# Strassen's seven products in the feed-forward of a decoder layer, with features on partitions from the output projection on

## The chip, the cores and the metric

The kernel runs on one core of a Trainium2 chip. A core has a matrix engine (PE, with its weight loads shown as PEld), a vector engine (DVE), a scalar engine (ACT), a general engine (POOL) and SP, which here only issues transfers. They run at the same time, each through its own queue of instructions in order, and wait for each other by semaphores. Operands lie in a memory of 128 partitions (SBUF); PE writes into another (PSUM). The metric is the device time of one execution in microseconds; the number given is the median of the runs.

## The reference

One decoder layer over 1024 tokens of width 1024, in fp32:

```python
n = rms_norm(h, g_mix)
# projections of n, latent attention o_a, stick-breaking attention o_b
merged = sigmoid(gate_a) * (o_a @ w_br_mla) + sigmoid(gate_b) * (o_b @ w_br_sb)
h = h + merged @ w_out                                              # output projection
n2 = rms_norm(h, g_ffn)
h = h + (silu(n2 @ w_ffn_gate) * (n2 @ w_ffn_up)) @ w_ffn_down      # feed-forward, inner width 2816
e = rms_norm(p @ w_ple_proj, g_ple)                                 # per-layer embedding, p is 1024 x 256
h = h + sigmoid(h @ w_ple_gate) * e
return rms_norm(h, g_final)
```

## The kernel before

Every large product is made from fp32r operands of two parts. `split` (L102) writes the high part with a cast on ACT and the rest with a subtraction on DVE; `passes` (L106) issues three matmuls for each block of 128 inner rows: high by high, high by low, low by high. A matmul has 128 inner rows, 128 output rows and 512 output columns.

The stages follow each other: norm, input projections and stick-breaking attention up to about 562 us; latent attention up to about 820; the gated merge (`pb`); the output projection (`po`); then norm, feed-forward and per-layer embedding. From the output projection on, tokens lie on the partitions: `hres` is [128, 8 token tiles, 1024 features]. Since a product needs its inner dimension on the partitions, `transposed` (L124) turns tiles by 4 transposes on PE at a time (`tp`), and splits them: the normalised state before the feed-forward (`n2T`), the state and `p` before the per-layer embedding.

The feed-forward runs over 22 chunks of 128 inner features, in groups of 3, 4, 4, 4, 4 and 3. `gate_up` (L842) loads a column block of each weight, makes `pg` and `pu` for both halves of the tokens with 24 matmuls each, applies Silu on ACT and the product on DVE and splits the result into `gT`, which stays in SBUF. `down` (L860) then multiplies the group's `gT` with its rows of `w_ffn_down` for each token tile into `pd`, and DVE adds `pd` to `hres` (L866). The per-layer embedding follows the last group by three token tiles: `ple_e` (projection `pp`, its norm, transposes) and `ple` (gate product, addition, final norm, store).

The order of the instructions on each engine is set by the framework's scheduler, which simulates times and honours the priorities and the numbers of buffers given for each tile name (`bufs`); SP issues nearly all loads and stores, in order, and one that waits holds back those behind it. POOL issues the stores of the gates and branches and does powers, some multiplications and sums. PSUM has eight banks of 128x512, handed out in turn.

Of the kernel before, what the change touches and what calls it, by code (L numbers as in the profile page):

```python
# [10 lines left out]
F32 = mybir.dt.float32  # L11
# [40 lines left out]
def decoder_layer(ctx: ExitStack, tc: tile.TileContext, x, p, positions, g_mix, w_in, g_q_a, w_q_b,  # L52
                  g_kv_a, w_kv_b, w_br_mla, w_br_sb, w_out, g_ffn, w_ffn_gate, w_ffn_up, w_ffn_down,
                  w_ple_gate, w_ple_proj, g_ple, g_final, out):
    nc = tc.nc
    x, p, out = x[0], p[0, 0], out[0]
# [16 lines left out]
    d_oT = dram.tile([2, 512, S], F32, name="d_oT")  # L73
    d_freq = dram.tile([1, 64], F32, name="d_freq")
    d_rope = dram.tile([64, S], F32, name="d_rope")

# [4 lines left out]
    ident_r = const.tile([P, P], F32R, name="ident_r")  # L81
# [7 lines left out]
    incl = const.tile([P, P], F32R, name="incl")  # L89
    rest = const.tile([P, P], F32R, name="rest")  # L90
    mask_sb = const.tile([P, P], F32R, name="mask_sb")
    mask_mla = const.tile([P, P], F32R, name="mask_mla")

    def tri(tmpm, t, base_val, fill, sign, base):
        # base_val where sign * (row - column) + base >= 0, fill elsewhere
# [10 lines left out]
    def passes(ps, prods, first=True, last=True):  # L106
        n = len(prods)
        for i, ((ah, al), (bh, bl)) in enumerate(prods):
            nc.tensor.matmul(ps, lhsT=ah, rhs=bh, start=first and i == 0, stop=False)  # L109
            nc.tensor.matmul(ps, lhsT=ah, rhs=bl, start=False, stop=False)  # L110
            nc.tensor.matmul(ps, lhsT=al, rhs=bh, start=False, stop=last and i == n - 1)  # L111
# [12 lines left out]
    def transposed(ps_pool, spec, src, dst_h, dst_l, n):  # L124
        # src [128, n*128] -> dst[:, 0:n, :] split
        for c in range(0, n, 4):
            m = min(4, n - c)
            tp = ps_pool.tile([P, 512], F32, name="tp", **spec())
            for i in range(m):
                nc.tensor.transpose(tp[:, i * P:(i + 1) * P], src[:, (c + i) * P:(c + i + 1) * P], ident)  # L130
            tv = tp[:, 0:m * P].rearrange("p (a b) -> p a b", b=P)
            nc.scalar.copy(out=dst_h[:, c:c + m, :], in_=tv)
            nc.vector.tensor_tensor(out=dst_l[:, c:c + m, :], in0=tv, in1=r32(dst_h[:, c:c + m, :]),
                                    op=ALU.subtract)
# [845 lines left out]
```

## Time and profile before

| | |
|---|---|
| median of 3 runs | 1811.73 us (1811.12 to 1811.78) |
| profiled execution, span | 1810.5 us |
| PE busy | 1761.1 us, 97% |
| DVE, ACT, POOL busy | 957.4, 766.6, 219.2 us |
| last matmul of the merge, about | 862 us |
| output projection | 862 to 953 us |
| first gate product | 955 us |
| last matmul of the kernel starts | 1798.7 us |

The profile is of one execution of its own; its span is 1.2 us below the median of the timed runs. A row of a group reads: line, engine, operation, output tile from input tiles, shape, count, then busy time and the mean of one in ns, then idle time of that engine ahead of it and what ended it. A row of the timeline begins with start and duration in us. The slices cut the span into 40 parts of 45.3 us, one digit each, in tenths of the time.

### The profile page before, as it was taken

The page shows a single profiled execution, that of the slowest core. Times are in us where ns is not written, and L with a number is a line of the kernel's source. Part 1 is how long each engine was busy: PE and PEld are TensorE (multiplying, and loading weights), DVE is VectorE, ACT ScalarE, POOL GpSimd, SP SyncE. Part 2 cuts the span into 40 slices and gives each one's busy share as a digit, 9 for nine tenths or more (in the row PEclk, how much of TensorE's full clock was granted, in tenths as well). Part 3 has the DMA queues.
Part 4 walks back from the last instruction along what each step waited for, and adds up shares of the span by engine and source line. Part 5 has one row for each costly group of instructions (what it writes and reads, how often), then busy time and mean ns, then how long its engine had stood idle before and what let it go on. Part 6 is the DMA issues. An engine that isn't in the chain of part 4 may idle for free.

```text
span 1810.5 us, 21501 instructions
## 1 busy us (share of the span) xinstructions
PE 1761.1 (97%) x8224; PEld 1453.3 (80%) x8224; DVE 957.4 (53%) x1641; ACT 766.6 (42%) x1467; POOL 219.2 (12%) x328
## 2 busy tenths in 40 slices
PE   6999999999998999998999999999999999999997
PEld 5888878888786888875888888888888888888885
DVE  6676788777885667777633232232232322325443
ACT  5275677766775767776323111021021021013332
POOL 2021220000211433334100000000000000000111
PEclk9999999999999999999999999999999999999998
DMA  5211122213315111217531111021021021112011
GB/s 169 65 58 42 53 59 59 65 50 97 105 42 158 54 59 36 65 47 268 179 112 57 47 59 47 24 70 47 24 70 49 22 82 51 38 64 91 30 41 39
DMA packets 124377, 126.31 MB, mean 70 GB/s; under 512 B 14130, under 2 KB 100146, under 8 KB 124274
## 3 DMA queue, kind: packets, MB, share of 16 engines
q1 hardware_dynamic: 118242, 105.02, 19.2%
q0 software_dynamic: 6032, 19.93, 3.1%
q8 instruction: 64, 1.05, 0.2%
q14 instruction: 39, 0.32, 0.1%
HBM read 100.54 MB, written 23.60 MB: 69 GB/s over the span
## 4 chain that ended last, share of the span: by engine, by line
PE 59%; DVE 3%; issue 3%; ACT 2%; DMA 1%; POOL 1%; POOLq 0%; SPq 0%; DVEq 0%; ACTq 0%
PE pg L109 5%; PE pg L110 5%; PE pg L111 5%; PE pu L111 4%; PE pu L109 4%; PE pu L110 4%; PE pd L110 4%; PE pd L109 4%; PE pd L111 4%; PE tp L621 2%; PE po L110 1%; PE po L111 1%; PE po L109 1%; PE pb L109 1%; PE op L628 1%
## 5 line engine op out<-in xcount | busy, mean ns | idle before, releaser
L109 PE MATMUL pt<-nTh,w_h 128*128 128x512 f32 (+1 forms) x480 | 192.9, 403 | 3.3 <-ACT go L325 2.1
L110 PE MATMUL pt<-nTl,w_h 128*128 128x512 f32 (+1 forms) x480 | 190.4, 397 | 0.0
L111 PE MATMUL pt<-nTh,w_l 128*128 128x512 f32 (+1 forms) x480 | 189.4, 396 | 0.0
L103 ACT CAST w<-raw 128x1024 fp32r<-128x1024 f32 x73 | 75.0, 1047 | 262.5 <-PE pd L111 166.9
L104 DVE TENSOR_TENSOR w<-raw,w 128x1024 fp32r<-128x1024 f32 x73 | 88.4, 1223 | 135.7 <-ACT w L103 135.7
L856 DVE TENSOR_TENSOR sl<-pu,sl 128x512 f32<-128x512 f32 x44 | 30.4, 692 | 207.0 <-PE pu L111 207.0
L866 DVE TENSOR_TENSOR hres<-pd,hres 128x512 f32<-128x512 f32 x96 | 66.1, 690 | 137.8 <-PE pd L111 137.7
L111 PE MATMUL pg<-n2T,w 128*128 128x512 f32 x352 | 137.2, 390 | 0.0
L110 PE MATMUL pg<-n2T,w 128*128 128x512 f32 x352 | 137.2, 390 | 0.0
L109 PE MATMUL pg<-n2T,w 128*128 128x512 f32 x352 | 137.2, 390 | 0.0
L111 PE MATMUL pu<-n2T,w 128*128 128x512 f32 x352 | 137.2, 390 | 0.0
L109 PE MATMUL pd<-w,gT 128*128 128x512 f32 x352 | 137.2, 390 | 0.0
L111 PE MATMUL pd<-w,gT 128*128 128x512 f32 x352 | 137.1, 389 | 0.0
L110 PE MATMUL pu<-n2T,w 128*128 128x512 f32 x352 | 137.1, 389 | 0.0
L109 PE MATMUL pu<-n2T,w 128*128 128x512 f32 x352 | 137.1, 389 | 0.0
L110 PE MATMUL pd<-w,gT 128*128 128x512 f32 x352 | 137.1, 389 | 0.0
L115 POOL TENSOR_SCALAR rstd<-ms 128x1 f32<-128x1 f32 x32 | 7.5, 235 | 873.1 <-DVE ms L886 766.0
L109 PEld LDWEIGHTS pt<-nTh,w_h 128*128 128x128 f32 (+1 forms) x480 | 90.3, 189 | 26.0 <-ACT go L325 5.0
L111 PEld LDWEIGHTS pt<-nTh,w_l 128*128 128x128 f32 (+1 forms) x480 | 90.4, 188 | 20.4
L855 ACT ACTIVATE sl<-pg 128x512 f32<-128x512 f32 x44 | 26.3, 598 | 190.0 <-PE pg L111 190.0
L110 PEld LDWEIGHTS pt<-nTl,w_h 128*128 128x128 f32 (+1 forms) x480 | 90.5, 189 | 18.7
L607 POOL TENSOR_SCALAR pw<-pw,st 128x128 f32<-128x128 f32 (+5 forms) x48 | 75.5, 1580 | 71.3 <-DVE st L603 24.8
(333 smaller groups left out, 4154.4 us busy)
## 6 DMA issues: line engine op xcount, KB each, us to landing
w_raw<-w_in SPq DMA_DIRECT2D x33, 512.0 KB, 4.2
raw<-w_ffn_gate SPq DMA_DIRECT2D x22, 512.0 KB, 3.9
raw<-w_ffn_up SPq DMA_DIRECT2D x22, 512.0 KB, 3.9
raw<-w_ffn_down SPq DMA_DIRECT2D x22, 512.0 KB, 3.6
d_gate<-go POOLq DMA_DIRECT2D x32, 256.0 KB, 2.6
sg<-d_gate SPq DMA_DIRECT2D x16, 512.0 KB, 4.4
xt<-x SPq DMA_DIRECT2D x8, 512.0 KB, 5.3
d_br<-bo POOLq DMA_DIRECT2D x16, 256.0 KB, 2.4
```

Source lines behind the costliest of these rows:

```text
L103: nc.scalar.copy(out=h, in_=src)
L104: eng.tensor_tensor(out=l, in0=src, in1=r32(h), op=ALU.subtract)
L109: nc.tensor.matmul(ps, lhsT=ah, rhs=bh, start=first and i == 0, stop=False)
L110: nc.tensor.matmul(ps, lhsT=ah, rhs=bl, start=False, stop=False)
L111: nc.tensor.matmul(ps, lhsT=al, rhs=bh, start=False, stop=last and i == n - 1)
L115: nc.gpsimd.tensor_scalar(out=r, in0=ms, scalar1=EPS, scalar2=None, op0=ALU.add)
L607: nc.gpsimd.tensor_scalar(out=pw[:, 0:nk], in0=pw[:, 0:nk], scalar1=st[:, 6:7], scalar2=None, op0=ALU.mult)
L621: nc.tensor.transpose(tp[:, i * P:(i + 1) * P], rows[i][:, kb * P:(kb + 1) * P], ident)
L628: nc.tensor.matmul(op[:, c0:], lhsT=vst[:, kb, :], rhs=tl[:, c0:], start=False, stop=kb == last, skip_group_check=True)
L855: nc.scalar.activation(out=sl, in_=pg, func=AF.Silu)
L856: nc.vector.tensor_tensor(out=sl, in0=pu, in1=sl, op=ALU.mult)
L866: nc.vector.tensor_tensor(out=hres[:, t, cs], in0=pd, in1=hres[:, t, cs], op=ALU.add)
```

## The change

The layout is turned: from the merge on, features lie on the partitions and tokens in the columns, so `hres` is [128, 8 feature blocks, 1024 tokens]. The input x is also given transposed (`xT`), `p` only transposed (`pT`), and the output leaves transposed; the host turns it. All 144 transposes behind the attention go. The attention itself is unchanged.

- **Norms.** Sums over features are now sums over partitions. ACT squares each `hres` block, DVE sums the squares into `acc`, four one-column matmuls with a column of ones make the sum per token (`rstd_cols`, tile `pm`), POOL takes the power. `spread` turns that into a 128x512 tile in PSUM that holds the factor of each token in all partitions (`bc`), by four DVE operations and one fp32 matmul. The three gains are loaded as [128, 8] columns at the very start of the kernel.
- **Output projection.** The same 384 matmuls with operands exchanged. `hres` is loaded from `xT` ahead of it; the result is also stored to DRAM (`d_h`), since the norm overwrites `hres` in place.
- **Embedding projection** (`pp`, 96 matmuls) moves from the end to behind the output projection and is stored to DRAM (`d_e`).
- **Gate and up.** The weight's two blocks of 128 columns and two halves of the inner dimension, and the state's two halves of the inner dimension and of the tokens, make 2x2 blocks each. `right_factors` forms the state's sums once and splits all seven right-hand factors (`b1` to `b7`); `left_sums` forms a unit's four weight sums (`ws`) on POOL; `wino` splits each of seven left-hand factors (`wl`) and makes seven products of 12 matmuls in three PSUM tiles (1, 6, 7 and 4 are summed up in `pP`, 5 and 3 in `pQ`, 2 stands in `pR`), which ACT copies and DVE and POOL additions combine. 22 units of 84 matmuls replace 22 chunks of 96. The SwiGLU outputs (`c`) go to DRAM (`d_g`).
- **Down.** The same with the inner dimension in four groups of 2 x 3, 2 x 3, 2 x 3 and 2 x 2 blocks. For each group `hidden_factors` reloads pieces of `d_g` (`g`), forms differences on POOL (`t`, or in place in `g`) and splits them into tiles `b`, of which there are nine (`g` has ten, `t` four); four `down_unit`s each make seven products of 9 (last group 6) matmuls and add the results to `hres`: three through an ACT copy and a POOL addition, four by DVE from PSUM. `hres` is reloaded from `d_h` first.
- **End.** All of `hres` is split, then 16 gate products of 24 matmuls, the additions and squares, the final norm for each half of the tokens, and the stores.

```diff
+    gains = const.tile([P, 3, NK], F32, name="gains")
+    for gi, g in enumerate((g_ffn, g_ple, g_final)):
+        nc.sync.dma_start(out=gains[:, gi, :], in_=g.rearrange("o (k p) -> p (o k)", p=P))
...
+        for k in range(NK):
+            nc.sync.dma_start(out=hres[:, k, :], in_=xT[k * P:(k + 1) * P, :])
+        for k in range(4, NK):
+            wo_unit(wob, "woB", k, ew.tile([P, D], F32, name="raw", tag="raw", bufs=2))
...
+    def left_sums(sp, raw, nk, wide=4):
+        a11, a12, a21, a22 = blk(0, 0), blk(0, 1), blk(1, 0), blk(1, 1)
+        nc.gpsimd.tensor_tensor(out=s1, in0=a21, in1=a22, op=ALU.add)
+        nc.gpsimd.tensor_tensor(out=s2, in0=s1, in1=a11, op=ALU.subtract)
+        nc.gpsimd.tensor_tensor(out=s4, in0=a12, in1=s2, op=ALU.subtract)
+        nc.gpsimd.tensor_tensor(out=s3, in0=a11, in1=a21, op=ALU.subtract)
+        return {1: a11, 2: a12, 3: s4, 4: a22, 5: s1, 6: s2, 7: s3}
+    def right_factors(sp, dst, kk, b11, b12, b21, b22):
+        nc.gpsimd.tensor_tensor(out=t1, in0=b12, in1=b11, op=ALU.subtract)
+        nc.vector.tensor_tensor(out=t2, in0=b22, in1=t1, op=ALU.subtract)
+        nc.gpsimd.tensor_tensor(out=t3, in0=b22, in1=b12, op=ALU.subtract)
+        nc.vector.tensor_tensor(out=t4, in0=b21, in1=t2, op=ALU.subtract)
+        for i, src in ((5, t1), (6, t2), (7, t3), (3, b22), (4, t4)):
+            split(dst[i][:, 0, kk, :], dst[i][:, 1, kk, :], src)
+    ORDER = (1, 5, 2, 6, 7, 3, 4)
+    def wino(sp, left, right, nk, seen, wide=4):
+        def product(ps_t, i, first):
+            w = sp.tile([P, 2, wide, P], F32R, name="wl", tag="wl", bufs=3)
+            split(w[:, 0, 0:nk, :], w[:, 1, 0:nk, :], left[i])
+            passes(ps_t, [((w[:, 0, k, :], w[:, 1, k, :]), (right[i][:, 0, k, :], right[i][:, 1, k, :]))
+                          for k in range(nk)], first=first, last=i in (2, 3, 4), skip_group_check=True)
...
+            def done(f, t, c):
+                nc.sync.dma_start(out=d_g[(2 * j + f) * P:(2 * j + f + 1) * P, hcol(t)], in_=c)
...
+                if what in ("M1", "U2", "M5"):
+                    s[what] = wk.tile([P, HALF], F32, name="u", tag="u", bufs=3)
+                    nc.scalar.copy(out=s[what], in_=pt)
+                elif what == "C21":
+                    c = sl[1, 0]
+                    nc.vector.tensor_tensor(out=c, in0=pt, in1=c, op=ALU.mult)
+                    done(1, 0, c)
+                else:
+                    nc.vector.tensor_tensor(out=u, in0=pt, in1=u, op=ALU.add)
+                    nc.gpsimd.tensor_tensor(out=sl[key], in0=sl[key], in1=u, op=ALU.mult)
+                    done(*key, sl[key])
...
+                if what in ("M1", "U2", "M5"):
+                    nc.scalar.copy(out=s, in_=pt)
+                    nc.gpsimd.tensor_tensor(out=h, in0=s, in1=h, op=ALU.add)
+                else:
+                    nc.vector.tensor_tensor(out=h, in0=pt, in1=h, op=ALU.add)
+        for nk in (3, 3, 3, 2):
+            Bg = hidden_factors(k0, nk)
+            for j in range(4):
+                yield down_unit(j, k0, nk, Bg)
...
-    def transposed(ps_pool, spec, src, dst_h, dst_l, n):
-            def gate_up(fc):
-            def down(t, gTs, wd):
-            def ple_e(t):
-            def ple(t, e, hT):
```

The order on DVE between the output projection and the first products of the feed-forward, first before. `n2T` is the transposed state, `sl` and `gT` the feed-forward's values, L104 the subtraction of `split`:

```order
1181 L133 TENSOR_TENSOR n2T_9323<-tp,n2T_9323 128x4x128 x3
1182 L791 SCALAR_TENSOR_TENSOR gT<-hres,rstd,gf 128x1024
1183 L133 TENSOR_TENSOR n2T_9323<-tp,n2T_9323 128x4x128 x5
1184 L856 TENSOR_TENSOR sl<-pu,sl 128x512
1185 L104 TENSOR_TENSOR gT<-sl,gT 128x512
1186 L104 TENSOR_TENSOR w<-raw,w 128x1024
1187 L856 TENSOR_TENSOR sl<-pu,sl 128x512
1188 L104 TENSOR_TENSOR w<-raw,w 128x1024
```

In the change, the same place. L929 and L937 scale `hres` by gain and norm factor, L116 is the subtraction of `split`, L847 and L849 are DVE's sums in `right_factors`; `b_9598`, `b_9600` and `b_9603` are the factors `b1`, `b2` and `b3`:

```order
1192 L929 SCALAR_TENSOR_TENSOR hres<-hres,gains,bc 128x512 x8
1193 L116 TENSOR_TENSOR b_9598<-hres,b_9598 128x512
1194 L116 TENSOR_TENSOR wl<-raw,wl 128x512
1195 L116 TENSOR_TENSOR b_9598<-hres,b_9598 128x512 x3
1196 L116 TENSOR_TENSOR b_9600<-hres,b_9600 128x512 x4
1197 L937 SCALAR_TENSOR_TENSOR hres<-hres,gains,bc 128x512 x8
1198 L847 TENSOR_TENSOR ts<-hres,ts 128x512
1199 L116 TENSOR_TENSOR b_9603<-hres,b_9603 128x512
```

And further on in the same queue of the change, the last of 28 such sums and splits, up to the second product (`b_9599`, `b_9601`, `b_9602` and `b_9604` are `b5`, `b6`, `b7` and `b4`):

```order
1220 L847 TENSOR_TENSOR ts<-hres,ts 128x512
1221 L116 TENSOR_TENSOR b_9599<-ts,b_9599 128x512
1222 L849 TENSOR_TENSOR ts<-hres,ts 128x512
1223 L116 TENSOR_TENSOR b_9601<-ts,b_9601 128x512
1224 L116 TENSOR_TENSOR b_9602<-ts,b_9602 128x512
1225 L116 TENSOR_TENSOR b_9604<-ts,b_9604 128x512
1226 L116 TENSOR_TENSOR wl<-ws,wl 128x512
```

Before, eight subtractions stand between the last norm operation and the first value of the feed-forward. In the change the first left-hand factor's subtraction (`wl<-raw`) stands behind eight scalings and a split, and that of the second product (`wl<-ws` in the last row) behind all scalings, sums and splits of the right-hand factors.

The order on SP where the weights of the last group of down are issued, before. `raw` is a weight as loaded:

```order
140 L834 DMA raw<-w_ffn_gate 128x8x128
141 L834 DMA raw<-w_ffn_up 128x8x128
142 L836 DMA raw<-w_ffn_down 128x1024 x3
143 L929 DMA raw<-g_ple 128x1024
144 L934 DMA raw<-w_ple_proj 128x2x512 x2
145 L943 DMA raw<-w_ple_gate 128x2x512 x2
```

And in the change, from the last loads of gate and up to the first of down. `c` is a SwiGLU output, `g` a reloaded piece of it:

```order
155 L922 DMA raw<-w_ffn_gate 128x8x256
156 L975 DMA d_g<-c 128x512 x3
157 L922 DMA raw<-w_ffn_up 128x8x256
158 L975 DMA d_g<-c 128x512 x8
159 L1013 DMA g<-d_g 128x512 x15
160 L1047 DMA raw<-w_ffn_down 128x6x128
161 L1013 DMA g<-d_g 128x512 x2
162 L1047 DMA raw<-w_ffn_down 128x6x128
163 L1013 DMA g<-d_g 128x512 x3
```

Before, down's weights are loads like any others and depend on free buffers alone. In the change the last eight stores of `c`, and 15 reloads, stand ahead of down's first weights.

542 lines of the change are left out of this document (319 added, 223 removed).

## The prediction

> **What bounds the kernel now.** I read the head of the page first (busy time, slices, chain), then windows of the stages that the change touches, then single rows for prices.
>
> ```profile
> span 1810.5 us, 21501 instructions
> PE 1761.1 (97%) x8224; PEld 1453.3 (80%) x8224; DVE 957.4 (53%) x1641; ACT 766.6 (42%) x1467; POOL 219.2 (12%) x328
> PE   6999999999998999998999999999999999999997
> POOL 2021220000211433334100000000000000000111
> PE 59%; DVE 3%; issue 3%; ACT 2%; DMA 1%; POOL 1%; POOLq 0%; SPq 0%; DVEq 0%; ACTq 0%
> ...
> 820.00:870.00 50.00, 43.67 (x184) 33.52 (x183) 42.09 (x53) 30.96 (x40) 22.85 (x8) 1.00 0.80 276
> 870.00:955.00 85.00, 84.65 (x393) 69.93 (x392) 38.38 (x45) 23.53 (x35) 5.24 (x13) 1.00 0.44 136
> 1000.00:1200.00 200.00, 200.00 (x884) 165.63 (x883) 59.44 (x74) 31.27 (x41) 0.00 (x0) 1.00 0.17 50
> ```
>
> PE bounds it nearly everywhere; in the windows the columns are length, PE, PEld, DVE, ACT and POOL busy, granted clock, DMA share, GB/s. A typical stretch of the feed-forward has PE busy for 200 of 200 us and POOL for none. So a matmul removed there is time removed, and nothing there waits yet. One matmul costs its spacing, not its record:
>
> ```profile
> 1100.09 0.39 PE L110 MATMUL pg<-n2T,w 128*128 128x512 f32 x1
> 1100.32 0.39 PE L111 MATMUL pg<-n2T,w 128*128 128x512 f32 x1
> ...
> 928.71 1.47 PE L130 MATMUL tp<-ident,raw 128*128 128x128 f32 x12
> 929.94 0.48 PE L109 MATMUL po<-w,mT 128*128 128x512 f32 x1
> 930.26 0.39 PE L110 MATMUL po<-w,mT 128*128 128x512 f32 x1
> ```
>
> 200/884 gives 0.226 us a matmul. Twelve transposes and the product matmul behind them run from 928.71 to about 930.26, so a transpose takes (1.55 − 0.23)/12 = 0.11 us.
>
> **What is removed.** Of 2112 matmuls each, gate and up keep 22 units of 7 × 12 = 1848 together instead of 2112, and down 3 × 252 + 168 = 924 instead of 1056. That is 264 + 132 = 396 fewer: 396 × 0.226 = −89.6 us. The 144 transposes go: −15.8. Six single-pass fp32 products of 128x512 (`bc`) and 24 tiny ones are new: between 0.23 and four times that each, taken at the top, since fp32 isn't the split format: +5. PE's work falls by 100 us. All of it becomes time only if the other engines keep up; from here I price where they don't.
>
> **Prices for the other engines.**
>
> ```profile
> 838.17 4.28 POOL L738 TENSOR_TENSOR bb<-bb,sg 128x1024 f32<-128x1024 f32 x1 [6.86 <-ACT sg L734]
> 838.32 0.68 DVE L104 TENSOR_TENSOR wl<-raww,wh 128x512 fp32r<-128x512 f32 x1
> 838.92 0.68 DVE L104 TENSOR_TENSOR mT<-sg,mT 128x512 fp32r<-128x512 f32 x1
> 839.52 0.69 DVE L104 TENSOR_TENSOR wl<-raww,wh 128x512 fp32r<-128x512 f32 x1
> ...
> L738 POOL TENSOR_TENSOR bb<-bb,sg x8: 2394/2712/4284, 825.9 to 868.1; 128x1024 f32<-128x1024 f32 x8
> L744 DVE TENSOR_TENSOR sg<-sg,bb x16: 679/680/2896, 828.4 to 872.2; 128x512 f32<-128x512 f32 x16
> L345 POOL TENSOR_TENSOR sqa<-sqa,go x6: 1287/1294/1622, 124.0 to 230.0; 128x512 f32<-128x512 f32 x6
> L103 ACT CAST gT<-sl 128x512 fp32r<-128x512 f32 x44 | 27.2, 618 | 111.3 <-DVE sl L856 111.3
> L325 ACT COPY go<-pt 128x512 f32<-128x512 f32 x42 | 24.3, 578 | 20.6 <-PE pt L111 20.5
> L906 ACT ACTIVATE sg<-raw 128x512 f32<-128x512 f32 x16 | 10.1, 630 | 23.5 <-DVE raw L905 23.5
> L356 POOL TENSOR_TENSOR r<-r,mhalf 128x4 f32<-128x4 f32 x4 | 4.8, 1193 | 0.3
> L890 DVE SCALAR_TENSOR_TENSOR raw<-pp,rstd,raw 128x512 f32<-128x512 f32 x16 | 11.3, 747 | 8.0 <-POOL rstd L116 8.0
> L423 DVE TENSOR_TENSOR al<-sz,ah 128x384 fp32r<-128x384 f32 x16 | 8.9, 555 | 0.5
> L423 DVE TENSOR_TENSOR al<-sz,ah 128x256 fp32r<-128x256 f32 x16 | 6.7, 419 | 0.7 <-PE op L426 0.5
> ```
>
> The first four rows are the important ones. Three DVE subtractions with both operands in SBUF start 0.60 us apart, undisturbed, and the POOL sum beside them takes 4.28 us where its fastest twin takes 2.39: 1.89 longer, three times 0.6. In the other direction L744 takes 2.90 instead of 0.68 us where a POOL sum was ahead of it. So a POOL operation and a two-input DVE operation on SBUF exclude each other, and their times add. I call this sum the port time. Prices: POOL 128x512 1.29 us, DVE 0.60. Between 1.29 and 2.39 (128x1024) a line gives POOL 1.01 for 128x384 and 0.74 for 128x256; DVE takes 0.47 and 0.33 (555 and 419 ns, less the 0.09 by which a record is longer than the spacing).
>
> [...]
>
> **Start.** Three loads of gains with 4-byte elements are put first on SP's queue, ahead of the first `xt`, for which the first transpose waits.
>
> ```profile
> 3.23 3.44 SPq L155 DMA_DIRECT2D w_raw<-w_in  x2
> 6.72 3.83 SPq L262 DMA_DIRECT2D gcol<-g_q_a  x1
> ```
>
> 1024 pieces of w_in hold the queue for 1.72 us, 384 four-byte pieces for 3.83; each new load has 1024. Bounds 0 (the queue takes them quickly) and 12 (3 × 3.83); by piece count 3 × 1.72 = +5.
>
> **Merge to output projection.** The loads of `w_out` k=4 to 7 now stand behind 4 MB of `hres` from xT, which wait for the last merge product.
>
> ```profile
> raw<-w_out SPq DMA_DIRECT2D x8, 512.0 KB, 7.3
> xt<-x SPq DMA_DIRECT2D x16, 256.0 KB, 3.0
> out<-raw SPq DMA_DIRECT2D x16, 256.0 KB, 2.2
> ```
>
> At the 276 GB/s of the 820 to 870 window, 4 MB take 15 us, then 7.3 for a load and 2 for its split. The five output tiles that can begin on the first half of k give PE 60 × 0.226 = 13.6 us of cover, and the merge's tail uses some more. Bounds 2 and 12; I take +4.
>
> **Output projection to the first feed-forward products (A).** In the window 870 to 955 PE has 84.65 of 85 us, so before there is no stall here. Now, after the last output product, come the 16 projections `pp`: PE needs 96 × 0.226 = 21.8 us, but each passes two-deep buffers and takes ACT a cast of half a row (0.35), a copy (0.58) and a square (0.63): 16 × 1.56 = 25 on ACT, and with the filling of the first about 30. Their results go to `d_e` by SP; that and the 16 stores to `d_h` are 8 MB in a stretch with the DMA engines at 0.44, and nothing waits for them until the per-layer embedding. Then DVE's queue holds, in order: 8 scalings (0.69 each, 5.5), 9 subtractions (5.4), 8 scalings (5.5), and 28 two-input operations (16.8) that build the right-hand factors, all ahead of the weight subtraction of the *second* product. POOL's eight differences and the first weight sums share the port with these: +8. With the norm chain (copy 0.58, square 0.63, POOL's sum 1.29, then two short steps: 3.2), the broadcast (1) and the second product's sum, cast and subtraction (2.6) that is 78 us, of which PE works 26.5. So +51. Bounds: 38 (POOL hidden, projections at PE's pace) and 60.
>
> **Gate and up (B).** A pair of units is 168 matmuls, 38.0 us. Port: 11 POOL operations × 1.29 + 14 DVE subtractions × 0.60 = 22.6. DVE's seven additions with one operand in PSUM (0.6 each) bring its own time with all waits for the port to 27; ACT's 14 casts, 6 copies and 4 Silu are 15. All fit into 38. New on SP are the 88 stores to `d_g`, which wait for POOL's products and hold back the weight loads behind them; those have three buffers and are due a whole unit (19 us) later, so I cost them at nothing, and they come into the open once POOL is a unit late. The U2 to U3 reuse of a bank is covered by one product of 2.7 us, as long as DVE is not caught behind POOL twice. Bounds 0 and 15; +5.
>
> **Down (C).** A group of nk=3 is 252 matmuls, 57.0 us. POOL does 12 differences and 12 additions to `hres` (24 × 1.29 = 31.0) and 16 weight sums (16 × 1.01 = 16.2); DVE 21 splits (12.6) and 28 weight splits (28 × 0.47 = 13.2); its 16 additions with an operand in PSUM don't count. Port: 73 us, more than PE. The nk=2 group: POOL 20 × 1.29 + 16 × 0.74 = 37.6, DVE 8.4 + 9.2 = 17.6, together 55 against 38.0. The four groups take 3 × 73 + 55 = 274 us; PE needs 209. At the start the last d_g store waits for the last product, 15 reloads stand behind it on SP, then the first weights: store 2.2, load 3.0, split and first operations about 5, with PE idle; at the end an addition. With these 11 us and 2 for the last additions, +78. Bounds: +17 if POOL and DVE did not exclude each other (only the start and the burst of each new group remain), +100 if the nine `b` buffers push the building of a group into the last unit of the one before.
>
> **End.** The 16 splits of `hres` start only after the last additions: +3. After the last product there are now norm, broadcast, eight scalings through three buffers and eight stores.
>
> ```profile
> 1798.69 0.39 PE L111 MATMUL pg<-wpg,gT 128*128 128x512 f32 x1
> 1804.25 0.81 SPq L917 DMA_DIRECT2D out<-raw  x2
> ```
>
> Before, 11.8 us pass from the last product to the end of the span. Norm chain 5 (square, addition, POOL's power 1.19, three hand-overs), broadcast 2, 8 × 0.69, store 2.2 and 3 of waits for the buffers make 18: +7 (bounds 3 and 12).
>
> **Sum** against the profiled span: 1810.5 − 100.4 + 5 + 4 + 51 + 5 + 78 + 3 + 7 = 1863. The median of the runs is 1811.73, 1.2 above the span; I forecast 1864 us.
>
> **Rivals.**
> 1. *The port doesn't decide down.* If what the rows show is peculiar to the merge's 128x1024 operands, and POOL's sums run beside DVE's subtractions, POOL needs 47 and DVE 35 us of PE's 57 in a group of nk=3, and PE sets the pace again. It decides once a group's 73 falls below 57. Then C is 17 instead of 78 and A loses its 8: 1795, faster. For it speaks that only few rows show the collision; against it, that they show it in both directions and by the full duration.
> 2. *Everything is hidden*, the starts too: 1811.7 − 100 + about 15 for start and end = 1726. It needs A below 10, where DVE's queue alone is 33 us; nearly excluded.
> 3. *Worse:* short waits at each product lower the granted clock, or DVE's additions from PSUM stand behind blocked subtractions so that waits add instead of overlapping, in gate and up too. At 7% more in gate, up and down (423 + 287 us as forecast) it is 1914. Against it: in the window 820 to 870 PE idles 6.3 of 50 us and the clock stays 1.00. [...]
>
> **Chances.** Forecast 0.64, rival 1 0.20, rival 2 0.04, rival 3 0.12. The forecast's own range is 1830 to 1890. For 8 in 10 I go down to rival 1 and up past the upper bounds: 1785 to 1900. Differences within 0.2% (3.6 us) can't be told from no change: faster 0.24, same 0.03, slower 0.73.
>
> **What would show it.** Right: POOL busy some 35 to 60% from gate/up on; a hole of 45 us in PE between the output projection and the second gate product; `hres<-s` and `t<-g` on POOL well above 1.29 us; a group of down taking about 73 us with PE below 80%; gate and up at 38 us a pair. Wrong: PE above 95% in down, or a pair of gate and up above 42 us.

## The result: 3.9% slower, 1884.52 us against 1811.76

The change takes 1884.52 us in the median of four runs (1876.36 to 1884.90), the kernel before 1811.76; the ratio is 1.039, 95% interval 1.037 to 1.041. Forecast were 1864 us, with 1785 to 1900 as range. The profiled execution has a span of 1874.7 us, 64.2 more than the one of before; its own time, 1876.36, was the lowest of the four.

The head of the page of the change, the lines that answer to those shown of before:

```profile
span 1874.7 us, 22421 instructions
PE 1713.2 (91%) x7744; PEld 1391.4 (74%) x7744; DVE 1211.1 (65%) x1962; ACT 940.4 (50%) x1818; POOL 624.2 (33%) x577
PE   6999999999999999988994799999999587999895
POOL 2021310001213333323024444344433688776200
PEclk9999999999999999989996799999999788999998
PE 73%; issue 10%; DVE 9%; POOL 3%; ACT 3%; DMA 3%; SPq 0%; POOLq 0%; DVEq 0%; ACTq 0%
```

PE has two holes, at the 22nd to 23rd and at the 32nd slice, and stays below 9 tenths up to the 34th, the first half of down; the granted clock falls at the same places (0.68 over the first hole and 0.91 over down, by the windows below). POOL is busy from the first hole to the end of down. The windows of the stages (length, then busy time of PE, PEld, DVE, ACT and POOL, clock, DMA share, GB/s):

```profile
864.00:959.00 95.00, 90.25 (x393) 74.32 (x392) 37.56 (x51) 20.29 (x30) 6.25 (x3) 0.96 0.39 141
959.00:1043.00 84.00, 42.79 (x138) 29.12 (x136) 55.90 (x80) 41.96 (x80) 38.08 (x26) 0.68 0.48 158
1043.00:1465.00 422.00, 419.22 (x1836) 346.12 (x1836) 164.89 (x231) 153.29 (x263) 170.23 (x120) 0.99 0.23 75
1465.00:1756.00 291.00, 234.90 (x926) 181.17 (x924) 242.80 (x268) 126.12 (x252) 216.02 (x156) 0.91 0.43 137
1756.00:1851.00 95.00, 92.31 (x399) 74.44 (x398) 62.20 (x91) 34.56 (x47) 1.02 (x1) 0.98 0.44 134
1851.00:1874.00 23.00, 4.20 (x12) 2.29 (x10) 13.09 (x23) 2.16 (x4) 1.01 (x1) 0.61 0.26 98
```

They are, in order: output projection; the stretch to the second gate product; gate and up; down; the gate products of the embedding; the tail. Matmuls of gate and up that wait for nothing start 0.2267 us apart on the average. With that for each matmul, a stage's time beyond its products is its hole:

| stage | length | products | hole | forecast |
|---|---|---|---|---|
| start (first output product at 864.0, before 862.5) | | | 1.6 | 5 |
| output projection | 95.0 | 384 = 87.0 | 8 | 4 |
| to the second gate product (A) | 84.1 | 26.5 | 58 | 51 |
| gate and up (B) | 422.1 | 1836 = 416.2 | 6 | 5 |
| down (C) | 290.4 | 924 = 209.4 | 81 | 78 |
| start of the end | 3.1 | | 3 | 3 |
| gate products of the embedding | 92.4 | 384 = 87.0 | 5 | 0 |
| tail beyond the one of before | 23.6 | (before 11.8) | 12 | 7 |

The holes sum to 175, forecast were 153. By count PE has the 396 products and 144 transposes less that were forecast. With the forecast's 100 us for that, 175 − 100 is some 10 us more than the 64 measured; by difference, that is what before had of small holes of its own outside the tail.

In down POOL and DVE alternate. Rows of the timeline of the change:

```profile
1548.06 4.89 DVE L116 TENSOR_TENSOR b<-g,b 128x512 fp32r<-128x512 f32 x3
1548.95 3.45 POOL L1058 TENSOR_TENSOR hres<-s,hres 128x512 f32<-128x512 f32 x2
...
L1058 POOL TENSOR_TENSOR hres<-s,hres x48: 1276/1612/3202, 1492.7 to 1747.6; 128x512 f32<-128x512 f32 x48
L116 DVE TENSOR_TENSOR b<-g,b x44: 674/1486/1783, 1471.1 to 1703.5; 128x512 fp32r<-128x512 f32 x44
L836 POOL TENSOR_TENSOR ws<-raw,ws 128x512 f32<-128x512 f32 x22 | 28.7, 1304 | 26.6 <-DVE wl L116 26.5
```

Three of DVE's subtractions, 0.6 us each alone, take 4.89; in the median such a subtraction takes 1.49 us where the fastest takes 0.67, and POOL's addition 1.61 where the fastest takes 1.28. The last row is gate and up, where POOL's weight sums take 1.30 on the average and so seldom collide. POOL's 33 multiplications there seem to collide more: they take 1.73 on the average where the fastest takes 1.28. But POOL and DVE have time to spare in this stage, and B came out near its forecast.

### The profile page after: what moved, and what is told of

The parts are those of the page before. It is cut to its first block, busy times and chain, and to the rows that moved or that the text cites. A ratio compares the mean times of both kernels' runs of the same rounds, so it can differ in the third digit from the quotient of the medians.

```text
span 1874.7 us, 22421 instructions
## 1 busy us (share of the span) xinstructions
PE 1713.2 (91%) x7744; PEld 1391.4 (74%) x7744; DVE 1211.1 (65%) x1962; ACT 940.4 (50%) x1818; POOL 624.2 (33%) x577
## 4 chain that ended last, share of the span: by engine, by line
PE 73%; issue 10%; DVE 9%; POOL 3%; ACT 3%; DMA 3%; SPq 0%; POOLq 0%; DVEq 0%; ACTq 0%
PE pP L123 6%; PE pP L121 6%; PE pP L122 6%; PE pt L121 5%; PE pt L122 5%; PE pt L123 5%; DVE b L116 3%; PE pQ L123 3%; PE pQ L121 3%; PE pQ L122 3%; PE tp L621 1%; PE pR L123 1%; PE pR L122 1%; PE pR L121 1%; PE po L121 1%
## 5 line engine op out<-in xcount | busy, mean ns | idle before, releaser
L121 PE MATMUL pP<-b,wl 128*128 128x512 f32 x528 | 212.5, 403 | 37.1 <-ACT wl L115 20.5
L123 PE MATMUL pP<-b,wl 128*128 128x512 f32 x528 | 212.3, 404 | 17.6 <-DVE wl L116 17.6
L116 DVE TENSOR_TENSOR wl<-ws,wl 128x512 fp32r<-128x512 f32 (+2 forms) x152 | 125.8, 829 | 142.4 <-ACT wl L115 141.8
L122 PE MATMUL pP<-b,wl 128*128 128x512 f32 x528 | 211.9, 401 | 0.0
L121 PEld LDWEIGHTS pP<-b,wl 128*128 128x128 f32 x528 | 102.5, 194 | 64.4 <-ACT wl L115 24.1
L116 DVE TENSOR_TENSOR wl<-raw,wl 128x512 fp32r<-128x512 f32 (+2 forms) x114 | 98.1, 863 | 64.8 <-ACT wl L115 64.5
L115 ACT CAST wl<-ws 128x512 fp32r<-128x512 f32 (+2 forms) x152 | 85.9, 565 | 105.2 <-PE pP L123 42.0
L123 PEld LDWEIGHTS pP<-b,wl 128*128 128x128 f32 x528 | 102.6, 194 | 45.7 <-DVE wl L116 23.6
L121 PE MATMUL pQ<-b,wl 128*128 128x512 f32 x264 | 104.5, 396 | 28.5 <-ACT wl L115 28.5
L122 PEld LDWEIGHTS pP<-b,wl 128*128 128x128 f32 x528 | 102.3, 194 | 22.0 <-DVE b L116 0.5
L115 ACT CAST wl<-raw 128x512 fp32r<-128x512 f32 (+2 forms) x114 | 64.4, 566 | 101.8 <-PE pP L123 53.4
L123 PE MATMUL pQ<-b,wl 128*128 128x512 f32 x264 | 104.2, 395 | 3.9 <-DVE wl L116 3.9
L122 PE MATMUL pQ<-b,wl 128*128 128x512 f32 x264 | 103.8, 393 | 0.0
L326 POOL DMA_DIRECT2D d_gate<-go x32 | 17.7, 554 | 257.8 <-ACT go L325 208.0
L1058 POOL TENSOR_TENSOR hres<-s,hres 128x512 f32<-128x512 f32 x48 | 76.7, 1603 | 19.0 <-ACT s L1057 17.2
```

What stands on the lines that cost most here:

```text
L115: nc.scalar.copy(out=h, in_=src)
L116: eng.tensor_tensor(out=l, in0=src, in1=r32(h), op=ALU.subtract)
L326: nc.gpsimd.dma_start(out=dst, in_=go[0:rows, :])
L1058: nc.gpsimd.tensor_tensor(out=h, in0=s, in1=h, op=ALU.add)
```

## The experiments

The theory is that of the prediction, called "port": an operation of POOL and one of DVE with two operands in SBUF exclude each other, so their times add, and in down that sum is more than PE's. Its main rival is "side by side": the two work in parallel, and PE waits for buffers and order. Times compare with 1884.5 for the change; the stages of the profiles are compared too, since executions differ by a few us in the unchanged first stage (below).

**All of POOL's work in down to DVE.** The other differences and the weight sums change engine in the same way; they are left out of the diff.

```diff
-                        nc.gpsimd.tensor_tensor(out=src, in0=piece(kb, 1), in1=src, op=ALU.subtract)
+                        nc.vector.tensor_tensor(out=src, in0=piece(kb, 1), in1=src, op=ALU.subtract)
...
-                if what in ("M1", "U2", "M5"):
-                    nc.scalar.copy(out=s, in_=pt)
-                    nc.gpsimd.tensor_tensor(out=h, in0=s, in1=h, op=ALU.add)
-                else:
-                    nc.vector.tensor_tensor(out=h, in0=pt, in1=h, op=ALU.add)
+                nc.vector.tensor_tensor(out=h, in0=pt, in1=h, op=ALU.add)
```

> In down alone, all that POOL did goes to DVE: the 12 differences and 16 weight sums of a group as DVE operations, and all 28 additions to hres straight from PSUM (so three ACT copies of a unit go too). Theory 'port' (POOL's and DVE's two-input operations on SBUF exclude each other, their times add): DVE alone needs 21 x 0.60 + 12 x 0.60 + 28 x 0.47 + 16 x 0.47 + 28 x 0.60 = 57 us for a group of nk=3, where POOL and DVE together needed 73; down falls from 290 us to 245 to 260, the kernel to 1840 to 1855. Rival 'side by side' (the two engines work beside each other, and the stall comes from buffers and order): DVE goes from 35 to 57 us a group and nothing is won; down 290 to 310, the kernel 1880 to 1905.

Measured: 1858.96 us, down 1465.0 to 1731.0, 266 us instead of 290. One engine does alone, and sooner, what two did. That speaks for the port and against the rival, though 6 us of the gain that was expected at least are missing. The edit also drops ACT's 48 copies and with them a hand-over from PE to ACT to POOL; the next run tells how much of the gain comes with these.

**Only the additions to DVE.** The second half of the edit above; POOL keeps differences and weight sums.

> As the change, but down's 48 additions of POOL to hres are made by DVE straight from PSUM (their ACT copies go too); POOL keeps differences and weight sums. Theory 'port': POOL's 12 x 1.29 = 15.5 us a group leave the port, additions with an operand in PSUM don't need it, so 73 becomes 57, as much as PE needs: down falls from 290 to 262 to 272, close to the run with all on DVE. Rival 'side by side': DVE's own work grows from 35 to 43 us a group, nothing won: 288 to 294.

Measured: 1864.74 us, down 274 us (1469.6 to 1743.4). Two thirds of the gain come with these 48 operations and the copies ahead of them. The last third, 8 us, comes when nothing but POOL's differences and weight sums go to DVE: no copy is dropped in that step. POOL's operations are also longer than DVE's (1.28 and 0.67 us at the fastest), which these runs do not separate from the port; the lengthened rows above show the port itself. On DVE the additions read PSUM, and none of these was lengthened beside POOL: in the change, where POOL is busy for 216 of the 291 us of down, DVE's additions take 0.69 us at most, also the 35 that run almost wholly during an operation of POOL (32 of all in this row, in ns):

```profile
L1060 DVE TENSOR_TENSOR hres<-pP,hres x32: 675/678/692, 1513.3 to 1756.0; 128x512 f32<-128x512 f32 x32
```

The windows from 1480 to 1720 show POOL's busy time fall from 190.73 to 135.51 while DVE's rises by 2 us only, though it does 58 operations more. In order: the change, only the additions, all on DVE, plain down (the run after the next):

```profile
1480.00:1720.00 240.00, 204.64 (x806) 159.35 (x807) 205.11 (x216) 103.46 (x206) 190.73 (x138) 0.91 0.43 136
...
1480.00:1720.00 240.00, 205.89 (x838) 161.06 (x839) 206.85 (x274) 90.62 (x178) 135.51 (x103) 0.93 0.46 145
...
1480.00:1720.00 240.00, 218.16 (x891) 170.15 (x892) 213.23 (x394) 93.26 (x185) 0.00 (x0) 0.96 0.45 142
...
1480.00:1720.00 240.00, 239.55 (x1051) 197.83 (x1049) 170.74 (x251) 50.12 (x75) 0.00 (x0) 0.99 0.27 91
```

DVE's count of operations goes from 216 to 394 while its busy time goes from 205 to 213 us: much of the 205 was waiting for POOL.

**All on DVE, and the four weight sums of a unit left out.** The diff is against the run with all on DVE.

```diff
-            yield from wino(wk, left_sums(wk, raw, nk, 3, nc.vector), right, nk, seen, 3)
+            yield from wino(wk, plain_left(raw, nk), right, nk, seen, 3)
```

> As the run with down on DVE alone, but down's four weight sums of each unit are left out (the products take the raw blocks), so part of the computation is missing. There down took 266 us instead of the 245 to 260 expected. If DVE, now with 57 us of work for a PE of 57 a group, is what binds, 16 x 0.47 = 7.5 us a group less give down about 240 (start 17, clock and group changes stay), the kernel 1832 to 1838. If the change of groups binds (nine b tiles, so that the next group's factors can't be built ahead), the weight sums don't matter: 262 to 266, the kernel 1855 to 1859.

Measured: 1846.2 us, down 255 us. Neither number: DVE's work counts, and 45 us remain of which it explains little. The profile has them as the start (18 us until the first product), gaps of 3 to 4 us where a group ends, and matmuls at the lower clock (14 us of them at 0.40 to 0.45 us each instead of 0.227, of which 6.6 are lost).

**Down by plain products.**

```diff
+        for k0 in range(0, NFF, 2):
...
+                    passes(pd, [((w[:, 0, kk, fs], w[:, 1, kk, fs]), (bs[kk][:, 0, hcol(hf)], bs[kk][:, 1, hcol(hf)]))
+                                for kk in range(2)])
+                    h = hres[:, f, hcol(hf)]
+                    nc.vector.tensor_tensor(out=h, in0=pd, in1=h, op=ALU.add)
```

> Down without Strassen, in the turned layout: 11 groups of two chunks, d_g reloaded by 512 KB, 96 plain matmuls a group, 16 DVE additions from PSUM; 1056 matmuls instead of 924, no POOL. Theory 'port': PE needs 239 us, DVE 14 of 21.8 us a group, so PE sets the pace; with about 10 us at the start down takes 250 instead of 290, the kernel about 1843. Rival 'reloads' (the way through DRAM and SP's order hold PE): the same bytes are reloaded, down stays at 280 or more, the kernel above 1872. Rival 'Strassen pays at PE's pace' would have this 30 us slower: above 1905.

Measured: 1842.73 us, down 252 us, PE busy for 239.55 of 240 us (the last row above). With 132 matmuls more, down is 38 us shorter. The reloads through DRAM, the same bytes, don't hold PE.

**The eight differences of the right-hand factors to DVE.**

```diff
-        nc.gpsimd.tensor_tensor(out=t1, in0=b12, in1=b11, op=ALU.subtract)
+        nc.vector.tensor_tensor(out=t1, in0=b12, in1=b11, op=ALU.subtract)
...
-        nc.gpsimd.tensor_tensor(out=t3, in0=b22, in1=b12, op=ALU.subtract)
+        nc.vector.tensor_tensor(out=t3, in0=b22, in1=b12, op=ALU.subtract)
```

> In right_factors alone, POOL's eight differences go to DVE. Theory 'port': POOL's 8 x 1.29 = 10 us leave the port and DVE gets 8 x 0.6 = 5 more, so the hole between the output projection and the second gate product falls from 84 to about 79 us. Rival 'side by side': DVE's queue only grows, the hole is 89 us. The kernel 1880 or 1889.

Measured: 1881.7 us; from the output projection's end to the second gate product 84.0 us, as in the change (84.1), and to the end of gate and up 503.3 against 506.2. Neither theory's number, though the port is at work in both. In the change POOL's first two differences ran in 1.27 us beside scalings that read PSUM; the later ones collided, and up to the second product six of DVE's operations took 1.74 to 1.76 us instead of 0.68, together 6.4 us longer. In the run DVE's list, eight operations longer, ends 4 us sooner. But the second product also needs POOL's first weight sum, and DVE's unbroken list now shuts that out. The change, then the run:

```profile
1040.77 1.65 POOL L834 TENSOR_TENSOR ws<-raw 128x512 f32<-128x512 f32 x1 [1.23 <-DVE b L116]
1043.27 3.45 POOL L834 TENSOR_TENSOR ws<-raw 128x512 f32<-128x512 f32 x1 [36.05 <-DVE b L116]
```

Counted from the end of the output projection, both sums end after 83.3 us. The edit took away one wait for the port and made another.

**The factors one after the other.** The loops over blocks and factors are exchanged, with all sums on DVE.

```diff
-        for kk in range(4):
...
-            right_factors(wk, Bn, kk, hres[:, kk, 0:HALF], hres[:, kk, HALF:], hres[:, kk + 4, 0:HALF],
-                          hres[:, kk + 4, HALF:])
+        for i in (5, 6, 7, 3, 4):
+            for kk in range(4):
...
+                split(Bn[i][:, 0, kk, :], Bn[i][:, 1, kk, :], src)
```

> The right-hand factors are built one factor after the other (b5, b6, b7, b3, b4 for all four blocks) instead of block by block, with all sums on DVE, so that the second product need not wait for the last block of all seven. Theory 'order on DVE' (the second product stands behind 28 operations): it starts after 8 of them, some 12 us earlier, but the products behind it then run at DVE's pace of 4.8 us a factor instead of 2.7, so 8 to 10 us remain, the kernel about 1875. Rival 'amount' (what counts is when the last factor is ready, as the first units need all seven): 0 to 3 us, 1882 to 1884.

Measured: 1872.51 us. The second product starts at 1023.9, 62 us after the output projection's end instead of 84, and the stretch up to the end of gate and up is 495.2 us instead of 506.2. Some 3 of these 11 us came already with the differences on DVE (503.3, the run before); 8 go with the order in DVE's queue. The other half of the earlier start is lost again, since the products now wait for one factor after the other.

**The embedding projection behind down.** The block of the projection, moved as it is:

```diff
-        with tc.high_priority(offset=-130):
-            for hf in range(2):
...
     with ExitStack() as pl:
         wk = pool(pl, "ple")
+        for hf in range(2):
...
+                passes(pp, [((w[:, 0, k, :], w[:, 1, k, :]), (pw[:, 0, k, :], pw[:, 1, k, :])) for k in range(2)])
```

> The 96 matmuls of the embedding projection go from behind the output projection to the stage behind down (their tiles come from that stage's pools); all else as in the change. Behind the output projection they took 37.6 us instead of PE's 21.8, and the building of the right-hand factors waited for them. Theory 'order': the hole before the second gate product falls from 84 to about 46 us, and at the end they cost 22 to 30, since PE can go on with the gate products while they wait: the kernel 8 to 16 us faster than the change, 1868 to 1876. Rival 'the work itself is slow' (cast, copy, square and reloads of 16 small pieces set its pace wherever it stands): at the end it takes 38 as well, nothing won, 1884.

Measured: 1880.9 us (1872.3 to 1887.9). A is as short as expected: to the end of gate and up 468.8 us instead of 506.2. But the end grows by as much: from down's last product to the last gate product 136.9 us instead of 95.3. That is what the rival expected: the projection costs 37 to 42 us wherever it stands, nearly twice PE's 21.8.

**Its weight loaded as a whole**, in the projection's old place: two splits instead of 16.

```diff
-                    nc.sync.dma_start(out=wraw, in_=w_ple_proj[:, f * P:(f + 1) * P].rearrange("(k p) n -> p k n", p=P))
...
+            for k in range(2):
+                wraw = ew.tile([P, D], F32, name="wraw", tag="raw", bufs=2)
+                nc.sync.dma_start(out=wraw, in_=w_ple_proj[k * P:(k + 1) * P, :])
+                split(w[:, 0, k], w[:, 1, k], wraw)
```

> As the change, but w_ple_proj is loaded and split once as a whole in its place behind the output projection. Forecast for this stretch were 30 us (ACT's cast, copy and square of each piece), measured 37.6. Theory 'buffers' (each piece waits for its load of some 2 us through two buffers, and the idle PE falls to the lower clock): 24 to 28 us, the kernel 10 to 13 us faster than the change, about 1872. Rival 'ACT' (copy and square, 1.2 us each, and POOL's sums of 1.29): 32 to 37, the kernel 1879 to 1884.

Measured: 1878.37 us. The projection takes 30 us instead of 37.6, between the two, and the wait behind it grows by 4 (to POOL's sums and the norm), so that A is 81 us. The small loads and splits cost 7.5 us; they were half of what was too much.

**hres loaded behind w_out.**

```diff
-            wo_unit(wob, "woB", k, ew.tile([P, D], F32, name="raw", tag="raw", bufs=2))
+            wo_unit(wob, "woB", k, ew.tile([P, D], F32, name="raw", tag="raw", bufs=4))
+        for k in range(NK):
+            nc.sync.dma_start(out=hres[:, k, :], in_=xT[k * P:(k + 1) * P, :])
```

> The loads of hres from xT are issued behind the loads of w_out k=4 to 7, which get four buffers instead of two. If the 8 us that PE lacks between merge and output projection come from w_out standing behind 4 MB of hres, the output projection ends some 6 us earlier, the kernel about 1878. If the loads of w_out were late for another reason (buffers freed late, DMA full from the merge), 1883 to 1885.

Measured: 1876.86 us; the output projection takes 88.0 us instead of 95.0 (868.7 to 956.7), its products alone 87.0. The hole is the order on SP's queue: in the change PE has one long wait in this stage, 4.7 us for the cast of the first weight behind `hres`, and runs at the lower clock after it (matmuls 0.43 us apart for 3.9 us; 0.66 granted from 880 to 890). The edit gives more buffers too, but for this first weight two were enough.

**Strassen in gate and up alone**: plain down, hres behind w_out, the projection at the end, the factors one after the other.

> Four edits together: down by plain products, hres loaded behind w_out, the embedding projection at the end, the right-hand factors one after the other. Strassen remains in gate and up alone. If the single gains add (42 for down, 7.6 for the loads, 8 to 16 for the projection, 8 for the factors), 1808 to 1818, about the kernel before. If the edits take the same time from each other (the holes behind the output projection overlap), 1820 to 1830.

Measured: 1827.67 us. The four single gains are 42, 7.6, 3.6 and 12, together 65; the sum of edits brings 57. Whether edits act on the same hole is not shown by that: counted in the profiles from the first output product to the end, the four are 39, 4, −2 and 7, together 48, and the sum of edits brings 56. Executions of one kernel differ by up to 8 us here (below), which is as much as the two ways do.

**The combination with three more edits**: the projection's weight as a whole, the first half of the tokens scaled during the second half of the output projection, eight tiles for the last scalings.

```diff
             rstd_cols(ew, acc, r_ffn[:, 4 * hf:4 * hf + 4])
+            if hf == 0:
+                bc = spread(ew, r_ffn[:, 0:4])
+                for k in range(NK):
...
-                o = wk.tile([P, HALF], F32, name="o", tag="e", bufs=3)
+                o = wk.tile([P, HALF], F32, name="o", tag="o", bufs=8)
```

> The combination of four edits (Strassen in gate and up alone) with three more: w_ple_proj is loaded and split once as a whole instead of 32 pieces of 128 KB, the first half of the tokens is scaled by its norm during the second half of the output projection, and the last scalings get eight output tiles instead of three. If the projection then runs at PE's pace (22 instead of 47 us at the end, where part ran beside gate products: 10 to 16 us), the scaling leaves DVE's queue behind the output projection (7 us), and the tiles save 2, the kernel takes 1802 to 1810, faster than the kernel before. If ACT's copies and squares set the projection's pace, and the start of the products waits for the second half anyway, 1818 to 1825.

Measured: 1812.28 us; ratio to the kernel before 0.9995, interval 0.9986 to 1.0004: the same time, not the faster one expected. Its stages from the output projection on:

```profile
866.50:955.20 88.70, 88.70 (x395) 73.17 (x393) 42.11 (x60) 21.93 (x35) 5.99 (x3) 1.00 0.35 133
955.00:1010.00 55.00, 32.32 (x99) 22.10 (x98) 45.73 (x70) 22.63 (x40) 22.30 (x9) 0.69 0.44 139
1010.00:1410.00 400.00, 399.12 (x1762) 330.28 (x1761) 152.89 (x219) 144.97 (x249) 159.85 (x113) 1.00 0.24 78
1410.00:1662.00 252.00, 242.21 (x1060) 199.59 (x1058) 168.08 (x242) 47.45 (x68) 0.00 (x0) 0.98 0.28 98
1662.00:1789.00 127.00, 118.05 (x509) 95.18 (x509) 79.42 (x115) 61.45 (x96) 22.76 (x17) 0.97 0.49 158
1789.00:1809.00 20.00, 4.68 (x14) 2.56 (x12) 11.34 (x21) 1.86 (x3) 1.01 (x1) 0.58 0.28 105
```

Gate and up keeps PE busy for 399 of 400 us with 12.5% fewer matmuls: while it runs, Strassen's saving of 60 us is whole. What remains of the price stands before it (55 us with some 22 of products), at the seams and in the tail, and takes all of it.

**The seam to down.** Down's weights and reloads get memory that comes free early, and POOL issues the stores to `d_g`.

```diff
-                nc.sync.dma_start(out=d_g[(2 * j + f) * P:(2 * j + f + 1) * P, hcol(t)], in_=c)
+                nc.gpsimd.dma_start(out=d_g[(2 * j + f) * P:(2 * j + f + 1) * P, hcol(t)], in_=c)
...
-    cp = pool(cs_, "right2")
+    cp = pool(cs_, "right2", side="right")
```

> The seven edits, with two more at the seam from gate and up to down, where PE still idled 12 us, and at the seam to the embedding, 7.6 us: down's weights and reloads lie over factors that are used first in a unit (so over memory that comes free early), and the stores to d_g are issued by POOL behind its products, so that SP's loads for down stand behind no store. If the seams are a matter of queue and memory, 10 to 16 us go, 1797 to 1802, faster than the kernel before. If the last SwiGLU output must go through DRAM first anyway, or POOL's weight sums now wait behind a store, 1808 to 1816.

Measured: 1811.08 us; ratio 0.9988, interval 0.9978 to 0.9998, about 0.1% faster than before at the most likely. The first product of down now follows the last of gate and up by 1.1 us in the records instead of 9.8, but down's last product starts no earlier (1662.6, against 1661.7 in the run before; 0.7 us earlier if counted from the first output product). Two us go in the first group of 96 matmuls, which waits inside: 25.9 us instead of 24.2. Each of the ten groups behind it takes 22.4 us instead of 21.8, though PE is busy all the time and the clock is 1.00 in both. The run before, then this one:

```profile
1440.00:1640.00 200.00, 200.00 (x884) 165.61 (x883) 136.70 (x197) 34.74 (x49) 0.00 (x0) 1.00 0.21 70
1440.00:1640.00 200.00, 200.00 (x859) 160.88 (x858) 131.07 (x187) 33.79 (x46) 0.00 (x0) 1.00 0.21 71
```

A matmul takes 0.2333 us here instead of 0.2267. That costs 7 us in down and 2 in the gate products of the embedding, and eats the gain of the seam. The stages at this pace are those whose factors lie in the pool that was moved; gate and up, whose factors were not, keeps 0.2267. Why matmuls are slower from there was not tried.

## Why the prediction was right, and where it was off

**What held.** The matmuls that PE loses, and the two places that cost more than it: A and down. Down was forecast at 287 us from prices of a trace that has only eight POOL sums of this kind, and took 290. The reason is shown by the lengthened rows and by the two runs that move POOL's work: DVE alone is faster than DVE and POOL together, and letting the additions read PSUM brings two thirds of it. In down of the change the 44 subtractions `b<-g`, with both inputs in SBUF, take 1.49 us in the median and up to 1.78 (the 33 of `b<-t` 0.68 in the median and up to 1.78), and the additions from PSUM 0.68 in the median and 0.69 at most.

Of the signs that the forecast named (in brackets), a pair of units of gate and up took 38.4 us (38), the hole before the second gate product was 58 (45), POOL's sums in down took 1.6 (well above 1.29) and POOL was busy 40% in gate and up (35 to 60) but 74% in down; PE was busy 81% there (below 80).

**But the sum of 73 us a group is not the whole of it.** From each group's first product to that of the next the four groups take 91, 72, 63 and 48 us, where 73, 73, 73 and 55 were forecast. That both sum to 274 is luck: a group was priced as if port and PE ran evenly, but the first took 18 us longer and the last two were shorter. The waits of PE in down, with what it waited for, total, times and the longest:

```profile
PE pP L121 <- ACT wl L115: 18.5, 4, 16.7
PE pP L123 <- DVE wl L116: 17.6, 11, 2.8
PE pP L121 <- DVE hres L1060: 15.5, 4, 5.2
PE pQ L123 <- DVE wl L116: 2.1, 5, 0.8
```

16.7 us are the start (forecast 11). The others are few and long: they stand mostly around the change from one group to the next, with several units at full pace in between (14.3 us for 63 products). The likely reading is that port and the nine `b` buffers act together: the next group's factors must be built while the last unit runs, and at that place POOL and DVE take turns. No run changed the number of buffers. The forecast named both, and priced the first alone.

**Rival 3 was partly true beside it.** After a long wait, here of 16.69 us, PE runs at about half pace:

```profile
1482.06 0.80 PE L121 MATMUL pP<-b,wl 128*128 128x512 f32 x1 [16.69 <-ACT wl L115]
...
1487.57 0.63 PE L123 MATMUL pP<-b,wl 128*128 128x512 f32 x1
1488.00 0.63 PE L121 MATMUL pP<-b,wl 128*128 128x512 f32 x1
1488.42 0.63 PE L122 MATMUL pP<-b,wl 128*128 128x512 f32 x1
```

The spacing is 0.427 us instead of 0.227. In A and in down the matmuls at this spacing (0.40 to 0.45) take 11.5 and 28.1 us, of which 5 and 13 are lost; the forecast had nothing for this. Against it the forecast set a row in which 6.3 us of short waits left the clock at 1.00. A stretch in the attention of before shows the lower clock, 0.57:

```profile
476.00:484.00 8.00, 6.60 (x20) 5.32 (x20) 7.94 (x13) 5.63 (x10) 3.50 (x7) 0.57 0.72 165
```

What sets the lower clock off is shown in part only. In down of the change, of eight gaps of 2.4 us and more between the starts of two matmuls (the start of down and gaps inside a slow stretch left out) seven were followed by half pace, and none of those from 0.7 to 2.0 us was. But in the row above the longest wait of PE is 1.4 us, so the length of a single wait does not decide it alone.

**The sum of 1.29 us for POOL** held: undisturbed sums took 1.26 to 1.30 in the change, so the row of before was the right price.

**Terms that were mis-sized.** The start: 1.6 us instead of 5; the loads of the gains held SP for 0.43 to 0.57 us each, not 1.72, and the first matmul starts 2.5 us later than before (10.6 instead of 8.1). With differences of up to 6 us ahead of the output projection (below) the 1.6 says little by itself. The output projection: 8 instead of 4; the term was there, the cover was overrated. The embedding projection: 37.6 us instead of 30, its loads and the lower clock not counted. The port's share in A: 8 forecast, 6.4 by the rows of DVE (above). The small products: some 18 us of PE in the change, where +5 was taken. Its top, four times 0.23 for a broadcast, was the author's assumption, which no row of before shows; in the change a sum over partitions takes 0.95 us and a broadcast 1.02 at full clock, but seven of the twelve ran at the lower clock and took 1.7 to 2.1. What goes beyond the 5 us stands in the holes of the table. The tail: 23.6 us instead of 18; in it the eight one-column matmuls and the broadcast alone take 1.9 and 2.1:

```profile
1850.86 0.39 PE L123 MATMUL pg<-b,wpg 128*128 128x512 f32 x1
1857.78 1.87 PE L707 MATMUL pm<-ones,acc 128*128 128x1 f32 x8 [6.53 <-DVE acc L1108]
1861.90 2.08 PE L718 MATMUL bc<-diag,ones_pp 128*128 128x512 f32 x2 [2.25 <-DVE diag L715]
```

Seven us pass before the first of them, while DVE finishes the embedding's additions: the wait is DVE's queue, not the norm. These misses mostly add up, to 22 us; that the forecast did not credit before with its own small holes, some 10 us, takes half of it back.

**What stays open.** The span of the profiled execution is 1874.7 us, but three of four timed runs are 8 us longer. In the profiles of the experiments, whose code is the same up to the merge, the first output product starts between 864.0 and 869.9, so up to 6 us of such differences arise in the attention or ahead of it. Why was not tried. The turned layout with plain products everywhere was not run either, so the saving of the transposes and the price of the layout are not separated from Strassen.

## What to carry to other kernels

A matmul saved is paid for by sums and splits on other engines: add up, stage by stage, what each group of them needs, and add POOL's time to that of DVE's operations with two operands in SBUF instead of taking the larger: in down of the change such a DVE subtraction (`b<-g`) took 1.49 us in the median, where the fastest took 0.67. Look also at where in a group the work falls: the sum was right over down, and wrong by up to 18 us for a single group. In down DVE alone did sooner what DVE and POOL did together, above all where an operand could be read from PSUM (0.69 us at most beside POOL). Here Strassen's saving came through where one set of right-hand factors serves many units (gate and up: 22 units, 399 of 400 us of PE busy) and not where each group of four units needs a new set (down). A stage that must be built whole before PE may start costs its building time and the clock behind it (A of the change: a hole of 58 us, and 0.68 granted); in the best run here these costs took all of the saving but 0.1% of the time.

## What the runs showed of the hardware that was not expected

- In down of the change, seven of eight gaps of 2.4 us and more between matmuls were followed by matmuls of 128x512 that came 0.427 us apart, for up to 4.3 us at a stretch, then 0.227 again; gaps of 0.7 to 2.0 us did not do this. In before, at 477 us, a wait of 1.4 us did.
- Matmuls of 128x512 came 0.2333 us apart instead of 0.2267, at a granted clock of 1.00 and without a wait, in the three stages whose factors lie in the pool that the last run moved: 859 instead of 884 in 200 us. The cause is open.
- A load of 1024 four-byte pieces held SP's queue for 0.43 to 0.57 us at the start of the kernel, where one of 384 pieces behind other loads held it for 3.3 to 3.8, so the number of pieces does not set it. Two loads of `w_in` of the same size held it for 0.47 and 3.41, one behind the other.
- DVE did 394 operations in 213 us of records where, beside POOL, 216 took 205: a record's length includes the time for which the engine is shut out, so that busy shares alone (63 of 70 us at the start of down) do not tell work from waiting.
